# A hybrid SSD and attention block: attention's gate projected by channels, its tiles in another pool, and norm scaling moved to ScalarE

## The chip, the cores and the metric

The kernel runs on one core of a Trainium2 chip. The metric is the device time of one execution in microseconds. TensorE (PE in the profile; PEld is its weight load) multiplies matrices from SBUF into PSUM, VectorE (DVE) and ScalarE (ACT) do elementwise work, GpSimd (POOL) a few small operations, and SyncE (SP) issues the DMAs.

## The reference

One layer, 1024 tokens of 1024 channels, float32. The input is normed and projected; one part goes through a state space scan (SSD), another through differential attention; both are gated, joined, projected out, added to the input and normed.

```python
proj = jnp.einsum('bsd,de->bse', rms_norm(h, norm_gain), w_in)
z_ssd, xbc, dt_raw, q, k, v, z_attn = jnp.split(proj, SPLITS, axis=-1)
...                                   # the scan gives y_ssd
# 8 heads, two maps m each, causal, with a linear bias by distance
p = softmax(where(dist >= 0, q @ k.T * 64**-0.5 - slope * dist, -inf))
w = p[:, :, 0] - lam * p[:, :, 1]
attn = rms_norm(w @ v, subln_gain) * (1.0 - lambda_init)   # over a head's 128 channels
y_attn = attn.reshape(bsz, seq, D_ATTN) * silu(z_attn)
h = h + concatenate([y_ssd, y_attn]) @ w_out
return rms_norm(h, final_norm_gain)
```

## The kernel before, in words

Every projection splits both factors into a high and a low float32r part (hi and lo of the weights, uh and ul of the normed input, which stands with channels on the partitions) and adds three products. `proj_tok` makes 128 tokens by 256 channels: the input is the stationary operand, and each of its 24 matmuls has 256 columns. `proj_ch` makes 128 channels by 512 tokens: the weights are stationary, and each of its 24 matmuls has 512 columns. Results go to one of two PSUM banks with the tag "mm".

After the scan's two groups, attention goes over four pairs p of heads (2p and 2p + 1). In program order a pair is: q and k of the even head (`proj_qk`), v of both heads (`proj_v`), attention of the even head in two halves of 512 tokens (`run`, `attend`), the gate's projection for both heads, q and k of the odd head, and its attention. In the last pair the gate's second half is projected after q and k of the odd head. The gate is silu(z) times two: Tanh on ScalarE (L321), then (tanh + 1) * z on VectorE (L322), in tiles `za` of 512 tokens by 256 channels.

`attend` takes four blocks of 128 queries: scores into PSUM (L557), maximum with bias on VectorE (L563), exponential on ScalarE (L581), combination of both maps on VectorE (L594), transposes on TensorE (L602), eviction on ScalarE (L605), product with v (L609). At the end of a half it leaves `oc`, queries on partitions, and the norm's factor `r` (L614 to L632).

`gate` multiplies `oc` by r and z (L641, per 128 queries), transposes (L647), evicts with the norm's gain g8 (L649), and stores to the DRAM tile `tt_d` (L651), from which the output projection loads its stationary operand. For the last head's first half it also writes hi and lo of the last of the 16 channel tiles (kt = 15) of three token tiles directly (L656, L657). Gates wait in a list and are made during a later half's blocks, at the places given by `at`.

The output projection (L709 to L711) needs the pieces of `tt_d`: `load_t` loads them to `rt` (L701) and splits them into th and tl (L703, L704). Token tiles 0 to 2 are begun while attention of the last head still runs; their loads stand in the program after the last gate projection, at a lowered priority.

Tiles come from SBUF pools by tag. G has 13 slots of 4 KB per partition: x, convolution outputs, `dist`, q and k (six tiles per head), v (two per pair), z, later `tts[2]`, `xr0` and most of the second half of w_out. K has 4 slots of 2 KB: small setup tiles, the scan's state and gate pairs, later `rt` and two residual tiles. H has 5 slots (`oc`, `t`, `tTa`). A planner takes the program with its own simulated costs, hands out slots, and fixes each engine's order before the run; each engine then works through its list, waiting on semaphores.

Of the kernel before, what the change touches and what calls it, by code (L numbers as in the profile page):

```python
# [8 lines left out]
F32 = mybir.dt.float32  # L9
F32R = mybir.dt.float32r  # L10
BF16 = mybir.dt.bfloat16
AF = mybir.ActivationFunctionType
ALU = mybir.AluOpType
AX = mybir.AxisListType

P = 128
# [4 lines left out]
HALF = 512  # L21
# [17 lines left out]
def kernel(  # L39
# [11 lines left out]
    V, A, G, T = nc.vector, nc.scalar, nc.gpsimd, nc.tensor  # L51
# [29 lines left out]
    def ps_mm():  # L81
        return psum.tile([P, HALF], F32, tag="mm", bufs=2, name="mm")
# [9 lines left out]
    def ps_t():  # L92
        return psum.tile([P, HALF], F32, tag="tp", bufs=1, name="tp")
# [66 lines left out]
    g8 = const.tile([P, 1], F32, name="g8")  # L160
# [17 lines left out]
    for half in range(2):  # L178
        for t in range(4 * half, 4 * half + 4):
            ss = sm.tile([P, 1], F32, tag="ss1", name=f"ssx{t}")  # L180
            A.activation(tH([P, D], BF16, "sqx"), x_t[t], AF.Square, accum_out=ss)
            r = rsqrt_mean(ss, 1, 1.0 / D, f"x{t}")
            V.tensor_scalar(x_t[t], x_t[t], r, None, ALU.mult)
        for d in range(ND):
            pt = ps_t() if d == 4 else ps_o() if d == 5 else ps_1()
# [17 lines left out]
    def proj_ch(w, n, half, ps):  # L203

        hi, lo = w
        cut = slice(n * P, (n + 1) * P)
        for d in range(ND):
            T.matmul(ps, hi[:, d, cut], uh[half][:, d, :], start=(d == 0), stop=False)  # L208
            T.matmul(ps, hi[:, d, cut], ul[half][:, d, :], start=False, stop=False)  # L209
            T.matmul(ps, lo[:, d, cut], uh[half][:, d, :], start=False, stop=(d == ND - 1))  # L210
# [113 lines left out]
    def proj_gate_half(w, half, name):  # L324
        z = tG([P, 4, 256], name=name)
        for a in range(2):
            proj_gate(w, 2 * half + a, z[:, 2 * a : 2 * a + 2, :])
        return z
# [5 lines left out]
    for d0, d1 in D3:  # L334
        hi, lo = (tG([P, d1 - d0, NZ], F32R, f"wz_{n}{d0}") for n in ("hi", "lo"))
        for n, raw in enumerate(raw_z0 + [wdt_raw]):
            cut = slice(n * P, min(NZ, (n + 1) * P))
# [186 lines left out]
    def proj_v(p):  # L524
# [9 lines left out]
            vs.append(v)  # L534
        return vs

    def attend(h, half, qkc, vs):

        qs, ks = qkc
        slope = 2.0 ** -(h + 1)  # L540
        vcut = slice((h % 2) * P, (h % 2 + 1) * P)
        po = ps_o()
        sums = sm.tile([P, 2, 4], F32, tag="sums", name=f"sums{h}{half}")
        for ii in range(4):
            i = 4 * half + ii
            n = (i + 1) * P
# [13 lines left out]
            for m in range(2):  # L560
                ps = pss[m]
# [5 lines left out]
                    op0=ALU.add,  # L567
                    op1=ALU.max,
                    scale=1.0,
# [16 lines left out]
                    scale=slope,  # L586
# [11 lines left out]
            for b0 in range(0, i + 1, 4):  # L598
                nb_ = min(4, i + 1 - b0)
                pt = ps_t()  # L600
# [12 lines left out]
        oc = tH([P, HALF], name=f"oc{h}{half}")  # L613
        V.tensor_scalar(oc, po, O_MAX, -O_MAX, ALU.min, ALU.max)  # L614
        ss = sm.tile([P, 4], F32, tag="ss4", name=f"sso{h}{half}")
        for ii in range(4):
# [4 lines left out]
                scale=2.0**-12,  # L621
# [6 lines left out]
        keep = sm.tile([P, 4], F32, tag="keep", name=f"keep{h}{half}")  # L628
        V.scalar_tensor_tensor(keep, ss, SQ_MAX, inv, op0=ALU.is_lt, op1=ALU.mult)
        V.tensor_scalar(ss, ss, SQ_MAX, None, ALU.min)  # L630
        r = rsqrt_mean(ss, 4, 2.0**24 / P, f"o{h}{half}")
# [1 line left out]
        yield oc, r  # L633

    def gate(h, half, normed, z):
        vcut = slice((h % 2) * P, (h % 2 + 1) * P)
        oc, r = normed
        tt = tH([P, HALF], name=f"t{h}{half}")
        for ii in range(4):
            cut = slice(ii * P, (ii + 1) * P)  # L640
            V.scalar_tensor_tensor(  # L641
                tt[:, cut], oc[:, cut], r[:, ii : ii + 1], z[:, ii, vcut], op0=ALU.mult, op1=ALU.mult
            )
        pt = ps_t()
        for ii in range(4):
            cut = slice(ii * P, (ii + 1) * P)
            T.transpose(pt[:, cut], tt[:, cut], ident)  # L647
        tT = tH([P, HALF], name=f"tTa{h}{half}")
        A.activation(tT, pt, AF.Copy, scale=g8)  # L649
        td, k = tt_of(8 + h, 4 * half)  # L650
        dma(td[k], tT)  # L651
        if h == HEADS - 1 and half == 0:
            for t in range(3):
                cut = slice(t * P, (t + 1) * P)
                hi, lo = (x[:, AHEAD_K - 1, :] for x in tts[t][1])
                A.activation(hi, pt[:, cut], AF.Copy, scale=g8)  # L656
                V.scalar_tensor_tensor(lo, pt[:, cut], g8, hi.bitcast(F32), op0=ALU.mult, op1=ALU.subtract)  # L657


    NK = 16  # L660
# [52 lines left out]
    waiting = []  # L713

    def run(h, half, qkc, vs, at):

        unit = attend(h, half, qkc, vs)
        for n in range(4):
            next(unit)
            if n in at and waiting:  # L720
                gate(*waiting.pop(0))
        return next(unit)

    for p in range(HEADS // 2):
        h = 2 * p
        qkc = proj_qk(h)
        vs = proj_v(p)
        even = [run(h, half, qkc, vs, (1,)) for half in range(2)]
        zw = load_w(B_ZA + 2 * p, B_ZA + 2 * p + 1, f"za{p}")
        last = p == HEADS // 2 - 1  # L730
        zs = [proj_gate_half(zw, half, f"za{p}{half}") for half in range(1 if last else 2)]
        qkc = proj_qk(h + 1)
        if last:
            zs.append(proj_gate_half(zw, 1, f"za{p}1"))
        waiting += [(h, half, even[half], zs[half]) for half in range(2)]
        if last:
            xr0 = tiles_out()
            with tc.high_priority(-2000):
                for t in range(3):
                    load_t(t, 0, 4)  # L740
                wo = [load_wo(0)]
        for half in range(2):
            at = (2,) if last and half else (2, 3)
            waiting.append((h + 1, half, run(h + 1, half, qkc, vs, at), zs[half]))
    while waiting:
        gate(*waiting.pop(0))

# [45 lines left out]
    for t in range(NT):  # L793
# [18 lines left out]
        for k, (n, c0, c1) in enumerate(pieces):  # L812
            if t <= 2 and n == 0:
                ps = pss[t]
            else:
                ps = ps_mm()
# [50 lines left out]
```

## Time and profile before

| | |
|---|---|
| median of three runs | 1049.15 us (1048.91 to 1049.41) |
| profiled execution, its own time | 1049.18 us |
| its span, first to last instruction | 1047.4 us |
| TensorE busy | 1021.0 us, 97% |
| VectorE, ScalarE, GpSimd busy | 586.8, 505.7, 114.2 us |
| granted TensorE clock | 0.999 |

Times in a timeline are microseconds from the start of the span. A matmul's duration runs from its start to its modelled end and overlaps the next one's. In a group's row the figures are count, busy time, mean duration in ns, and after the bar the idle time of that engine just before, with what ended it. The scan and what precedes it fill the span up to about 366 us, attention with its projections runs to about 914, and the rest of the output projection to the end.

### The profile page before, as it was taken

To read this page: it belongs to the slowest core of one execution; us is meant where nothing else is said; L and a number is where in the kernel's file an instruction comes from. 1 tells how busy PE (TensorE), PEld (TensorE's weight loads), DVE (VectorE), ACT (ScalarE), POOL (GpSimd) and SP (SyncE) were. 2 spreads that over 40 slices of the span, in tenths; PEclk is the share of its full clock that TensorE was granted. 3 is DMA by queue.
4 is the path that set the end of the run, shared out by engine and by line. 5 is a ranking of instruction groups with operands and counts; after the bars stand their busy time and mean duration, and the time that the engine had idled before them with its cause. 6 is when DMAs were issued, how large, how long until landed. Compare 5 with 4: busy or idle time off the path is not lost.

```text
span 1047.4 us, 16245 instructions
## 1 busy us (share of the span) xinstructions
PE 1021.0 (97%) x6334; PEld 906.2 (87%) x6334; DVE 586.8 (56%) x1285; ACT 505.7 (48%) x1137; POOL 114.2 (11%) x141
## 2 busy tenths in 40 slices
PE   6999999999999999999999999999999999999997
PEld 5988888879988998889998899988998987788886
DVE  6555678755666265573664745637546477462221
ACT  8354367834457354463554544534545565341110
POOL 6000024200223100000000000000002230010000
PEclk9999999999999999999999999999999999999999
DMA  7111224311224212320122121131211433463211
GB/s 291 41 63 41 68 65 131 91 51 61 101 81 121 81 42 61 81 67 25 51 61 61 41 62 62 51 81 41 62 56 52 136 116 129 141 182 115 81 46 41
DMA packets 52085, 84.54 MB, mean 81 GB/s; under 512 B 3932, under 2 KB 30633, under 8 KB 52009
## 3 DMA queue, kind: packets, MB, share of 16 engines
q1 hardware_dynamic: 52008, 83.51, 25.3%
q8 instruction: 50, 0.82, 0.3%
q14 instruction: 27, 0.21, 0.1%
HBM read 62.45 MB, written 12.65 MB: 72 GB/s over the span
## 4 chain that ended last, share of the span: by engine, by line
PE 89%; issue 3%; ACT 3%; DVE 2%; DMA 1%; POOL 1%; POOLq 0%; DVEq 0%; SPq 0%; ACTq 0%
PE mm L208 9%; PE mm L209 9%; PE mm L210 9%; PE mm L217 8%; PE mm L218 8%; PE mm L219 8%; PE mm L709 6%; PE mm L710 6%; PE mm L711 6%; PE o L609 5%; PE S L557 5%; PE S L439 3%; PE tp L602 3%; PE S L448 1%; PE S L452 1%
## 5 line engine op out<-in xcount | busy, mean ns | idle before, releaser
L563 DVE CUSTOM_DVE_ANT_0 s<-S,dist 128x256 f32<-128x256 f32 (+7 forms) x128 | 94.5, 755 | 111.2 <-PE S L557 103.9
L581 ACT ACTIVATE s<-s,small 128x256 f32<-128x256 f32 (+7 forms) x128 | 98.5, 770 | 72.1 <-DVE small L573 71.5
L208 PE MATMUL mm<-uh,hi_qk 128*128 128x512 f32 x256 | 101.5, 397 | 0.0
L210 PE MATMUL mm<-uh,lo_qk 128*128 128x512 f32 x256 | 101.0, 394 | 0.0
L209 PE MATMUL mm<-ul,hi_qk 128*128 128x512 f32 x256 | 100.8, 394 | 0.0
L557 PE MATMUL S<-k,q 128*128 128x512 f32 (+2 forms) x384 | 90.6, 355 | 0.5 <-DVE small L563 0.5
L605 ACT ACTIVATE wT<-tp 128x512 f32<-128x512 f32 (+2 forms) x96 | 46.6, 485 | 77.7 <-PE tp L602 77.2
L609 PE MATMUL o<-v,wT 128*128 128x128 f32 x576 | 79.9, 275 | 2.5 <-ACT wT L605 2.5
L609 PEld LDWEIGHTS o<-v,wT 128*128 128x128 f32 x576 | 74.3, 191 | 6.6 <-ACT wT L605 3.7
L217 PE MATMUL mm<-hi_v,uh 128*128 128x256 f32 x256 | 73.7, 288 | 0.9 <-DVE q L508 0.9
L218 PE MATMUL mm<-lo_v,uh 128*128 128x256 f32 x256 | 73.3, 286 | 0.0
L219 PE MATMUL mm<-hi_za,ul 128*128 128x256 f32 x256 | 73.2, 286 | 0.0
L219 PE MATMUL mm<-hi_v,ul 128*128 128x256 f32 x256 | 73.0, 285 | 0.0
L218 PE MATMUL mm<-lo_za,uh 128*128 128x256 f32 x256 | 72.9, 285 | 0.0
L217 PE MATMUL mm<-hi_za,uh 128*128 128x256 f32 x256 | 72.8, 284 | 0.0
L557 PEld LDWEIGHTS S<-k,q 128*128 128x128 f32 x384 | 64.6, 189 | 9.4 <-DVE small L563 1.4
L210 PEld LDWEIGHTS mm<-uh,lo_qk 128*128 128x128 f32 x256 | 48.1, 188 | 9.8 <-issue 0.2
L208 PEld LDWEIGHTS mm<-uh,hi_qk 128*128 128x128 f32 x256 | 48.1, 188 | 9.1 <-issue 0.2
L209 PEld LDWEIGHTS mm<-ul,hi_qk 128*128 128x128 f32 x256 | 48.2, 188 | 8.7
L217 PE MATMUL mm<-hi_z,uh 128*128 128x256 f32 x192 | 55.2, 287 | 0.0
L594 DVE SCALAR_TENSOR_TENSOR s<-s,small,s 128x128 f32<-128x128 f32 (+3 forms) x64 | 54.2, 848 | 1.6
L219 PE MATMUL mm<-hi_z,ul 128*128 128x256 f32 x192 | 55.0, 287 | 0.0
(217 smaller groups left out, 2631.5 us busy)
## 6 DMA issues: line engine op xcount, KB each, us to landing
m<-acs_d SPq DMA_DIRECT2D x16, 512.0 KB, 4.1
raw_qk<-in_w_blocks_dram SPq DMA_DIRECT2D x16, 512.0 KB, 4.0
q<-q SPq DMA_DIRECT2D x32, 256.0 KB, 2.9
rwo<-in_w_out_dram SPq DMA_DIRECT2D x16, 512.0 KB, 3.6
rt<-tt_d SPq DMA_DIRECT2D x27, 256.0 KB, 3.7
x<-in_x_dram SPq DMA_DIRECT2D x8, 512.0 KB, 6.2
raw_z<-in_w_blocks_dram SPq DMA_DIRECT2D x8, 512.0 KB, 4.1
raw_xs<-in_w_blocks_dram SPq DMA_DIRECT2D x8, 512.0 KB, 4.0
```

What stands on the lines that cost most here:

```text
L208: T.matmul(ps, hi[:, d, cut], uh[half][:, d, :], start=(d == 0), stop=False)
L209: T.matmul(ps, hi[:, d, cut], ul[half][:, d, :], start=False, stop=False)
L210: T.matmul(ps, lo[:, d, cut], uh[half][:, d, :], start=False, stop=(d == ND - 1))
L217: T.matmul(ps, uh[half][:, d, cut], hi[:, d, :], start=(d == 0), stop=False)
L218: T.matmul(ps, uh[half][:, d, cut], lo[:, d, :], start=False, stop=False)
L219: T.matmul(ps, ul[half][:, d, cut], hi[:, d, :], start=False, stop=(d == ND - 1))
L557: T.matmul(os[m], qs[half][m][:, part, qcut], ks[kh][:, m, :width], start=(part == 0), stop=(part == 1))
L563: V.tensor_tensor_reduce(out=s[:, :n], in0=ps[:, :n], in1=dist[:, S - n : S], op0=ALU.add, op1=ALU.max, scale=1.0, scalar=-3.0e38, accum_o ...
L581: A.activation(s[:, :n], s[:, :n], AF.Exp, bias=nb[:, m : m + 1], scale=slope, accum_out=sums[:, m, ii : ii + 1],)
L609: T.matmul(po[:, qcut], wT[:, kb, :], vs[kb // 4][:, kb % 4, vcut], start=(kb == 0), stop=(kb == i))
L709: T.matmul(ps, th[:, k, :], hi, start=(kt == first), stop=False)
L710: T.matmul(ps, th[:, k, :], lo, start=False, stop=False)
```

## The change

The gate's projection goes by channels: `proj_za` makes, for each head and half, 128 channels by 512 tokens with `proj_ch`, as two tiles per head. For the first three pairs the tiles are in pool K, for the last in G. In the last pair the even head's gate is projected before q and k of the odd head, and the odd head's after. Since z now has channels on partitions, `gate` scales `oc` by r alone, on ScalarE, transposes, and multiplies by g8 and z on VectorE as it evicts. The direct hi and lo of kt = 15 are taken from that result in SBUF rather than from PSUM.

```diff
+    def proj_za(w, n, name, keep):
+
+        z = []
+        for half in range(2):
+            z.append((tK if keep else tG)([P, HALF], name=f"{name}{half}"))
+            ps = ps_mm()
+            proj_ch(w, n, half, ps)
+            A.activation(z[half], ps, AF.Tanh, scale=0.5)
+            V.scalar_tensor_tensor(z[half], z[half], 1.0, ps, op0=ALU.add, op1=ALU.mult)
+        return z
...
     def gate(h, half, normed, z):
-        vcut = slice((h % 2) * P, (h % 2 + 1) * P)
         oc, r = normed
         tt = tH([P, HALF], name=f"t{h}{half}")
         for ii in range(4):
             cut = slice(ii * P, (ii + 1) * P)
-            V.scalar_tensor_tensor(
-                tt[:, cut], oc[:, cut], r[:, ii : ii + 1], z[:, ii, vcut], op0=ALU.mult, op1=ALU.mult
-            )
+            A.activation(tt[:, cut], oc[:, cut], AF.Copy, scale=r[:, ii : ii + 1])
...
         tT = tH([P, HALF], name=f"tTa{h}{half}")
-        A.activation(tT, pt, AF.Copy, scale=g8)
+        V.scalar_tensor_tensor(tT, pt, g8, z[half], op0=ALU.mult, op1=ALU.mult)
...
-                A.activation(hi, pt[:, cut], AF.Copy, scale=g8)
-                V.scalar_tensor_tensor(lo, pt[:, cut], g8, hi.bitcast(F32), op0=ALU.mult, op1=ALU.subtract)
+                A.activation(hi, tT[:, cut], AF.Copy)
+                V.tensor_tensor(lo, tT[:, cut], hi.bitcast(F32), ALU.subtract)
...
-        zs = [proj_gate_half(zw, half, f"za{p}{half}") for half in range(1 if last else 2)]
+        zs = [proj_za(zw, 0, f"za{h}", not last)]
+        if not last:
+            zs.append(proj_za(zw, 1, f"za{h + 1}", not last))
         qkc = proj_qk(h + 1)
         if last:
-            zs.append(proj_gate_half(zw, 1, f"za{p}1"))
-        waiting += [(h, half, even[half], zs[half]) for half in range(2)]
+            zs.append(proj_za(zw, 1, f"za{h + 1}", not last))
+        waiting += [(h, half, even[half], zs[0]) for half in range(2)]
...
-            waiting.append((h + 1, half, run(h + 1, half, qkc, vs, at), zs[half]))
+            waiting.append((h + 1, half, run(h + 1, half, qkc, vs, at), zs[1]))
```

## The prediction

> **What bounds the kernel now.** I read the busy times and the 40 slices of the page first, then the chain that ended last.
>
> ```profile
> span 1047.4 us, 16245 instructions
> PE 1021.0 (97%) x6334; PEld 906.2 (87%) x6334; DVE 586.8 (56%) x1285; ACT 505.7 (48%) x1137; POOL 114.2 (11%) x141
> PE   6999999999999999999999999999999999999997
> PE 89%; issue 3%; ACT 3%; DVE 2%; DMA 1%; POOL 1%; POOLq 0%; DVEq 0%; SPq 0%; ACTq 0%
> ```
>
> TensorE is busy in every slice and is nine tenths of the chain; VectorE and ScalarE are half idle. So what shortens TensorE's own list of work shortens the kernel, unless it only opens a hole elsewhere. Next I looked for the holes there are, in stretches of the attention phase (columns: stretch, its length, TensorE's busy time and instructions, granted clock, DMA share, GB/s).
>
> ```profile
> 455.00:470.00 15.00, 13.56 (x78) 1.00 0.30 89
> 590.00:604.00 14.00, 13.20 (x74) 1.00 0.21 59
> 725.00:739.00 14.00, 13.21 (x75) 1.00 0.23 66
> 835.00:870.00 35.00, 34.31 (x191) 1.00 0.31 98
> 870.00:892.00 22.00, 19.75 (x114) 1.00 0.42 135
> 892.00:914.00 22.00, 20.88 (x106) 1.00 0.45 156
> ```
>
> The first three are the seams between head pairs: 1.44, 0.80 and 0.79 us idle, 3.0 in all. The other three are the end of attention: 0.69 + 2.25 + 1.12 = 4.1 us idle. The clock was 1.00 throughout.
>
> **Part 1, the gate's projection.** By tokens it is 4 pairs x 8 token tiles x 24 = 768 matmuls of 256 columns. By channels it is 8 heads x 2 halves x 24 = 384 matmuls of 512 columns, the form that the q/k projection already has. A matmul's listed duration overlaps the next one's, so the price is the distance of starts (columns: start, duration, engine, line). The gate now:
>
> ```profile
> 367.01 0.28 PE L219 MATMUL mm<-hi_za,ul 128*128 128x256 f32 x1
> ...
> 369.17 0.28 PE L219 MATMUL mm<-hi_za,ul 128*128 128x256 f32 x1
> ```
>
> Eighteen steps in 2.16 us, 0.120 each. The q/k projection in an unbroken block, and where attention's work had just come between:
>
> ```profile
> 433.73 0.39 PE L209 MATMUL mm<-ul,hi_qk 128*128 128x512 f32 x1
> ...
> 437.36 0.39 PE L210 MATMUL mm<-uh,lo_qk 128*128 128x512 f32 x1
> ```
> ```profile
> 409.69 0.40 PE L208 MATMUL mm<-uh,hi_qk 128*128 128x512 f32 x1
> ...
> 411.99 0.39 PE L209 MATMUL mm<-ul,hi_qk 128*128 128x512 f32 x1
> ```
>
> Sixteen steps in 3.63 us, 0.227 each; ten in 2.30, 0.230 each. So 768 x 0.120 = 92.2 us becomes 384 x 0.227 = 87.2: **-5.0 us**. With 0.230 throughout it is -3.9, and no row is below 0.227. I take -5.0, since the 0.120 too comes from an unbroken block. The 384 weight loads that go as well lay under matmuls and are worth nothing by themselves; the matmuls were what filled the time.
>
> What a rule would make of it: the Trainium skill, "TensorE: Matmul & The Clock Gate", section "Back-to-back issue gap", gives a warm gap of N / 2.4 + 2.5 ns, so 109.2 ns for 256 columns and 215.8 for 512. By that estimate halving the count saves 83.9 - 82.9 = 1.0 us only. This trace shows about 13 ns beyond N / 2.4 at both widths, not 2.5, and the measured pitch decides.
>
> **Part 2, scaling and gating.** A gate before: four VectorE products, four transposes, one ScalarE copy out of PSUM. After: four ScalarE copies scaled by r, the same transposes, one VectorE product out of PSUM. The rows, first groups (their mean in ns after the comma), then two runs of four:
>
> ```profile
> L641 DVE SCALAR_TENSOR_TENSOR t<-oc,r_o,za 128x128 f32<-128x128 f32 x64 | 18.7, 353 | 0.1
> L649 ACT ACTIVATE tTa<-tp,g 128x512 f32<-128x512 f32 x16 | 10.9, 684 | 19.4 <-PE tp L647 19.4
> L322 DVE SCALAR_TENSOR_TENSOR za<-za,mm 128x512 f32<-128x512 f32 x16 | 10.9, 683 | 5.7 <-ACT za L321 5.7
> L425 ACT ACTIVATE m<-m,acs 128x128 f32<-128x128 f32 x128 | 39.3, 389 | 13.6 <-DMA m<-acs_d 13.6
> ```
> ```profile
> 864.61 1.13 DVE L641 SCALAR_TENSOR_TENSOR t<-oc,r_o,za 128x128 f32<-128x128 f32 x4
> 341.79 1.11 ACT L412 ACTIVATE tT<-o,sg 128x128 f32<-128x128 f32 x4
> ```
>
> Four VectorE products took 1.13 us. Four ScalarE copies with a per-partition scale took 1.11 us reading PSUM; reading SBUF, the nearest row is L425 with 389 ns each, so the four lie between 1.11 and 4 x 0.39 = 1.56. The move out of PSUM is 0.684 on ScalarE against 0.683 on VectorE (L322). A gate's own path changes by -0.02 to +0.43 us. VectorE loses 16 x (1.13 - 0.68) = 7 us of work and ScalarE gains 16 x (1.11 to 1.56 - 0.68) = 7 to 14 us. TensorE's matmuls hide both, with half of either engine idle: I take 0. If the cover were gone at every gate it would cost 16 x 0.43 = 7 us: the copies stand in ScalarE's queue before the next block's exponential (L581) and the eviction of the transposed weights (L605), for which TensorE's L609 waits. That bites only at the seams and the end. The projection's Tanh and product stay 16 and 16 of 128x512. No DMA is added; SP issues the stores of tTa at the same points.
>
> For the last head's first half, hi and lo of three token tiles now come from SBUF:
>
> ```profile
> 891.95 0.37 ACT L656 ACTIVATE th<-tp,g 128x128 fp32r<-128x128 f32 x1 [0.42 <-DVE tl L657]
> 892.35 0.35 DVE L657 SCALAR_TENSOR_TENSOR tl<-tp,g,th 128x128 fp32r<-128x128 f32 x1 [0.43 <-ACT th L656]
> ```
>
> Reading one PSUM tile, the two engines took turns, each waiting 0.42 us for the other. Two such waits of ScalarE can go (-0.8 us at best).
>
> **Part 3, where z lies.** Pool G (13 slots) held two z tiles per pair; pairs 0 to 2 now use pool K (4 slots, four z of half the size). Pair 3 holds four in G instead of two. What a slot of G is worth shows at a seam (two VectorE rows, then TensorE's first filler):
>
> ```profile
> 453.34 0.68 DVE L508 SCALAR_TENSOR_TENSOR q<-mm,q 64x512 fp32r<-64x512 f32 x1 [0.62 <-ACT q L507]
> ...
> 468.85 0.69 DVE L508 SCALAR_TENSOR_TENSOR q<-mm,q 64x512 fp32r<-64x512 f32 x1
> 469.60 0.39 PE L217 MATMUL mm<-hi_v,uh 128*128 128x256 f32 x1 [0.36 <-DVE q L508]
> ```
>
> Two parts of one q projection left PSUM 15.5 us apart. In G at that time, by the code: dist 1, v 2, z 2, four of the running head's q and k, four of the next head's: 13, full. The next head's last q and k tiles wait for the running half's q to be read; both "mm" banks stay taken, and v's projection starts only at 469.60. Without z in G exactly two slots are free. I expect two thirds of the seams' 3.0 us to go: **-2.0 us**, bounds -3.0 (all of it) and 0 (the head's own chain ends there anyway).
>
> In pair 3 the two extra tiles leave G only when head 6 has been gated. They stand before the loads of token tile 2 (G for hi and lo, K for the raw pieces), and the kt = 14 step at the end waits for K too:
>
> ```profile
> 867.26 0.81 SPq L701 DMA_DIRECT2D rt<-tt_d  x2
> 872.27 0.50 PE L709 MATMUL mm<-wo_hi,th 128*128 128x512 f32 x1 [0.53 <-ACT th L703]
> ```
>
> The loads go out behind head 6's gate and TensorE waits for them. Best case -0.8 (above); the other end, +9.5, is rival two. I take **+1.0 us**, near the lower end, since gate and load would be late by a copy or two only.
>
> Sum: -5.0 + 0 - 2.0 + 1.0 = -6.0. The profiled execution took 1049.2 us, 1.8 more than its span and level with the median of 1049.15: **1043.2 us**. All best ends together give -5.0 - 3.0 - 0.8 = -8.8, all worst ends -3.9 + 7 + 9.5 = +12.6.
>
> **Rivals.** *One, no gain.* The TensorE time that goes turns into idle time at the same seams, because attention's chain (VectorE maximum, ScalarE exponential, transposes) sets a pair's end. For it: the seams are idle now. Against it: only 3 us in three seams, and q/k blocks without any attention lie between. It gives -1 to 0 us, about 1048.5; the rule's 1.0 us saving would end there too, with little added chance, as its pitch is not the trace's.
>
> *Two, the end.* Raw pieces of token tile 2 fill K while they wait for G, so the kt = 14 pieces cannot be loaded at 867.26 but only after the last scores of head 7 are read, some 10 us later. TensorE then loses the cover of tile 2's 14 x 3 x 0.227 = 9.5 us of matmuls: -5.0 - 2.0 + 9.5 = +2.5, 1051.7. It decides from a delay beyond 7 us on. Against it: K's other pieces free two slots with the first copy.
>
> *Three, K is not idle.* Token tile 0's first pieces take two of K's slots long before they are used:
>
> ```profile
> 326.59 0.99 SPq L701 DMA_DIRECT2D rt<-tt_d  x2
> 821.62 1.96 ACT L703 ACTIVATE th<-rt 128x512 fp32r<-128x512 f32 x4
> ```
>
> If they keep those places, four z share two slots, the other two z hold both "mm" banks until gates free them, and q/k groups lose their double buffer: up to 12 groups x 2.7 us (two evictions each on ScalarE and VectorE in turn, as L649 and L322 4 x 0.68) = 33 us, half of it filled by attention, an estimate: -5 + 16 = +11, 1060. Against it, the planner seems to hand out slots in program order, in which z of pairs 0 to 2 stand before these loads:
>
> ```profile
> 399.01 0.14 DVE L632 TENSOR_TENSOR r_o<-r_o,keep 128x4 f32<-128x4 f32 x1
> ...
> 431.83 0.69 DVE L614 TENSOR_SCALAR oc<-o 128x512 f32<-128x512 f32 x1 [4.20 <-PE o L609]
> 432.56 1.14 DVE L641 SCALAR_TENSOR_TENSOR t<-oc,r_o,za 128x128 f32<-128x128 f32 x4
> ```
>
> The first gate's operands were ready at 399.2, yet its tile of pool H came only after that of the next half, which stands before it in the program. Then the loads simply start later, still before 821.
>
> *Four, more.* All seams and half of the end fill: -5.0 - 3.0 - 2.0 = -10, 1039.
>
> **How the numbers follow.** Forecast, 1041 to 1046: 0.60. Rival four 0.14, one 0.11, two 0.08, three 0.07. What a measurement of this kernel can tell from no change is 0.2%, 2.1 us. Faster 0.74 (forecast and four), same 0.11, slower 0.15. The range 1038.5 to 1049.5 leaves out rival two and three and a little of four, 0.19; the likeliest case alone is 1041 to 1046.
>
> **What would show it.** Right: gate matmuls as 384 rows of 128x512 at 0.227 from start to start; TensorE's busy time near 1016; v's filler directly behind the next head's last q/k with no L508 pair 15 us apart; four ScalarE copies of 1.1 to 1.6 us per gate; z written without waiting for a gate. Wrong: ScalarE's Tanh (L321) or VectorE's product of z waiting on K, q/k groups alone in one PSUM bank, the first loads of token tile 0 still at 326, the kt = 14 step far later behind head 6's gate, or L609 waiting longer for L605.

## The result, and the profile after

The changed kernel is slower: 1055.67 us median (1054.22 to 1056.65, six runs) against 1049.39 (1048.91 to 1050.78, six runs) for the kernel before on the same chip, ratio 1.0057, 95% interval 1.0044 to 1.0070. The prediction, 1043.2 in a range of 1038.5 to 1049.5, was wrong by 12.5 us and in its sign. The profiled execution has a span of 1054.3 us at a granted clock of 0.997, 6.9 us longer than before's. One execution further down, of e12_prio_pool, took 1460.38 us at a granted clock of 0.655; ratios leave it out.

The page of the changed kernel, the lines that answer to those of before:

```profile
span 1054.3 us, 15478 instructions
PE 1021.5 (97%) x5950; PEld 887.9 (84%) x5950; DVE 587.7 (56%) x1237; ACT 514.9 (49%) x1185; POOL 113.1 (11%) x141
PE   6999999999999999999999999999999988899997
PE 90%; DVE 3%; ACT 3%; issue 1%; DMA 1%; POOL 1%; SPq 0%; POOLq 0%; DVEq 0%; ACTq 0%
```

There are 384 fewer matmuls, and three slices, the 33rd to the 35th, have fallen from 9 to 8: the stretch from about 843 to 922 us. The windows of before again, and the three stretches that turn out to matter (columns as in the prediction: stretch, length, TensorE's busy time and instructions, granted clock, DMA share, GB/s):

```profile
455.00:470.00 15.00, 15.00 (x107) 1.00 0.35 111
590.00:604.00 14.00, 14.00 (x109) 1.00 0.24 76
725.00:739.00 14.00, 14.00 (x109) 1.00 0.15 50
807.00:819.00 12.00, 9.96 (x67) 1.00 0.30 86
835.00:870.00 35.00, 30.77 (x164) 1.00 0.43 139
870.00:892.00 22.00, 19.79 (x109) 1.00 0.44 141
892.00:914.00 22.00, 21.07 (x114) 1.00 0.45 156
914.00:918.00 4.00, 1.36 (x9) 1.00 0.17 66
918.00:922.00 4.00, 4.00 (x11) 0.57 0.00 0
```

The seams are full, as forecast. The end is not: 4.23 us idle in 835 to 870 (before 0.69), 2.64 in 914 to 918, and behind that a stretch at a clock of 0.57. The new gate projection and the gate's new steps:

```profile
503.12 0.40 PE L209 MATMUL mm<-ul,hi_za 128*128 128x512 f32 x1
...
506.78 0.39 PE L210 MATMUL mm<-uh,lo_za 128*128 128x512 f32 x1
```
```profile
L652 ACT ACTIVATE t<-oc,r_o 128x128 f32<-128x128 f32 x64 | 20.7, 389 | 3.8 <-DVE r_o L643 3.8
L658 DVE SCALAR_TENSOR_TENSOR tTa<-tp,g,za 128x512 f32<-128x512 f32 x16 | 12.0, 750 | 16.8 <-PE tp L656 16.5
```

Sixteen steps in 3.66 us, 0.229 each: the price of part 1 was right to one per cent. The pieces of part 2 cost about what was said: four copies 20.7 / 16 = 1.29 us, the product 0.750 instead of 0.683.

To see where the time went I use one measure for all kernels: the sum of what the distance between two successive matmul starts exceeds the usual one for their shape (0.111 us for 128 columns or fewer, 0.120 for 256, 0.125 for 272, 0.175 for 384, 0.227 for 512), in us. It counts idle time and matmuls slowed by a low clock alike, and it is uncertain by about 1, since some records are missing. Each column is one traced execution. The last row counts the stretches between 765 and 930 us in which the clock record of that trace has TensorE at half rate; each is 3.41 us long and so costs up to 1.7. (e13 and e15, which leave out some matmuls, come further down.)

| stretch | before | after | e1_pack | e3_pack_vec | e9_prio | e18 | e16 | e13 | e15 |
|---|---|---|---|---|---|---|---|---|---|
| 330 to 765 | 16.4 | 15.2 | 15.2 | 12.5 | 13.4 | 15.2 | 11.7 | 16.4 | 15.4 |
| 765 to 810 | 1.3 | 2.5 | 1.2 | 1.2 | 1.1 | 2.0 | 1.2 | 1.3 | 1.4 |
| 810 to 870 | 2.8 | 8.9 | 7.9 | 10.0 | 7.3 | 8.2 | 5.1 | 5.6 | 6.5 |
| 870 to 900 | 5.4 | 4.7 | 4.3 | 4.0 | 4.1 | 5.7 | 4.5 | 7.2 | 5.6 |
| 900 to 930 | 0.2 | 4.7 | 2.0 | 1.9 | 4.5 | 0.2 | 1.2 | 0.2 | 0.2 |
| half rate | 0 | 1 | 0 | 1 | 1 | 1 | 0 | 1 | 2 |

The gate projection's own steps, where one follows another, took 0.1197 us on the mean before and 0.2288 after, which makes 91.9 and 87.9 us. So about 4 us of work went (5.0 forecast), and 11 us came behind 765 us, from the last pair on: idle time, but for up to 1.7 us of half rate. Four links in the trace of the changed kernel account for it; the experiments test the first, the third and the fourth.

*Head 7's q and k wait for slots of G.* SyncE's queue (columns: start, length, queue, line, operation, count), the changed kernel:

```profile
787.14 14.25 SPq L511 DMA_DIRECT2D q<-q  x3
817.49 0.47 SPq L511 DMA_DIRECT2D q<-q  x1
828.16 2.72 SPq L699 DMA_DIRECT2D rwo<-in_w_out_dram  x2
```

The fourth copy of q comes at 817.49, though head 7's q and k matmuls were through at 807.5; both "mm" banks stay taken, and the window 807 to 819 has 2 us idle. The copies of the kernel before are no earlier:

```profile
814.85 0.47 SPq L511 DMA_DIRECT2D q<-q  x1
818.04 0.47 SPq L511 DMA_DIRECT2D q<-q  x1
```

But there head 7's q and k matmuls ran until 818.8, so TensorE had work while the copies waited. The changed kernel was 11 us ahead with these matmuls, and the lead was gone with the wait: head 7's gate projection starts at 819.05, the last gate half of the kernel before at 818.98.

*The first piece of w_out waits for head 7's gate.* Its hi and lo take the place of the input's first half, uh and ul. Projected by tokens, the last gate half read only the second half of the input; by channels every head's gate reads both. ScalarE's first copies of w_out, before and after:

```profile
803.88 1.99 ACT L693 ACTIVATE wo_hi<-rwo 128x1024 fp32r<-128x1024 f32 x2
```
```profile
824.59 2.01 ACT L702 ACTIVATE wo_hi<-rwo 128x1024 fp32r<-128x1024 f32 x2 [0.69 <-PE mm L209]
831.77 1.06 ACT L702 ACTIVATE wo_hi<-rwo 128x1024 fp32r<-128x1024 f32 x1 [3.68 <-DMA rwo<-in_w_out_dram]
843.11 1.06 ACT L702 ACTIVATE wo_hi<-rwo 128x1024 fp32r<-128x1024 f32 x1 [5.62 <-DMA rwo<-in_w_out_dram]
850.34 1.06 ACT L702 ACTIVATE wo_hi<-rwo 128x1024 fp32r<-128x1024 f32 x1 [3.68 <-DMA rwo<-in_w_out_dram]
```

*ScalarE then stands before these loads in its list*, 13 us in the three rows, and head 7's exponentials behind them.

*The last piece of w_out's second half takes the slot of head 7's second z tile*, which is free only after the gate's product, now behind the transposes. VectorE, then TensorE:

```profile
912.35 1.23 DVE L703 TENSOR_TENSOR wp_lo<-rwo,wp_hi 128x1024 fp32r<-128x1024 f32 x1 [1.04 <-ACT wp_hi L702]
915.20 0.75 DVE L658 SCALAR_TENSOR_TENSOR tTa<-tp,g,za 128x512 f32<-128x512 f32 x1 [1.62 <-PE tp L656]
916.52 1.22 DVE L703 TENSOR_TENSOR wp_lo<-rwo,wp_hi 128x1024 fp32r<-128x1024 f32 x1
```
```profile
917.79 0.60 PE L719 MATMUL mm<-wp_lo,th 128*128 128x512 f32 x1 [2.64 <-DVE wp_lo L703]
918.19 0.63 PE L720 MATMUL mm<-wp_hi,tl 128*128 128x512 f32 x1
918.62 0.63 PE L718 MATMUL mm<-wp_hi,th 128*128 128x512 f32 x1
```

Before, the four products stood ahead of that gate's transposes and the last two pieces followed at 909.80 without a gap:

```profile
908.74 1.14 DVE L641 SCALAR_TENSOR_TENSOR t<-oc,r_o,za 128x128 f32<-128x128 f32 x4
909.80 2.35 DVE L694 TENSOR_TENSOR wp_lo<-rwo,wp_hi 128x1024 fp32r<-128x1024 f32 x2
```

After the change TensorE waits 2.64 us and then starts matmuls 0.426 us apart instead of 0.227.

### The profile page after: what moved, and what is told of

The parts are those of the page before. It is cut to its first block, busy times and chain, and to the rows that moved or that the text cites. A ratio compares the mean times of both kernels' runs of the same rounds, so it can differ in the third digit from the quotient of the medians.

```text
span 1054.3 us, 15478 instructions
## 1 busy us (share of the span) xinstructions
PE 1021.5 (97%) x5950; PEld 887.9 (84%) x5950; DVE 587.7 (56%) x1237; ACT 514.9 (49%) x1185; POOL 113.1 (11%) x141
## 3 DMA queue, kind: packets, MB, share of 16 engines
q1 hardware_dynamic: 52008, 83.51, 25.2%
## 4 chain that ended last, share of the span: by engine, by line
PE 90%; DVE 3%; ACT 3%; issue 1%; DMA 1%; POOL 1%; SPq 0%; POOLq 0%; DVEq 0%; ACTq 0%
PE mm L208 12%; PE mm L209 12%; PE mm L210 12%; PE S L568 5%; PE o L620 5%; PE mm L218 5%; PE mm L219 5%; PE mm L217 5%; PE mm L718 5%; PE mm L720 5%; PE mm L719 5%; PE S L439 3%; PE tp L613 3%; PE S L448 1%; PE S L452 1%
## 5 line engine op out<-in xcount | busy, mean ns | idle before, releaser
L568 PE MATMUL S<-k,q 128*128 128x512 f32 (+2 forms) x384 | 93.8, 358 | 4.2 <-DVE small L574 4.1
L173 POOL TENSOR_SCALAR m_o<-sso 128x4 f32<-128x4 f32 x16 | 3.1, 193 | 504.8 <-DVE sso L641 389.6
L719 PE MATMUL mm<-wp_lo,th 128*128 128x512 f32 (+1 forms) x144 | 53.3, 370 | 2.6 <-DVE wp_lo L703 2.6
L218 PE MATMUL mm<-lo_z,uh 128*128 128x256 f32 x192 | 54.9, 286 | 0.0
```

Source lines behind the costliest of these rows:

```text
L218: T.matmul(ps, uh[half][:, d, cut], lo[:, d, :], start=False, stop=False)
L568: T.matmul(os[m], qs[half][m][:, part, qcut], ks[kh][:, m, :width], start=(part == 0), stop=(part == 1))
L719: T.matmul(ps, th[:, k, :], lo, start=False, stop=False)
```

## The experiments

Times are medians; ratios are to the kernel before on the same chip, with their 95% intervals. The theories are named by letters in the expectations. A: pair 3's two extra tiles in G make the loss, by what then waits for slots. B: the scaling copies on ScalarE hold up what stands behind them. C: the planner made a worse order of the new work, by chance. P, formed after the first runs: the last pair is bound by the attention of heads 6 and 7, so that TensorE time saved turns into idle time there.

**e1_pack**: both halves of a head's z in one 4 KB slot, so pair 3 takes two slots of G, not four.

```diff
+        both = None if keep else tG([P, 2, HALF], name=name)
...
-            z.append((tK if keep else tG)([P, HALF], name=f"{name}{half}"))
+            z.append(tK([P, HALF], name=f"{name}{half}") if keep else both[:, half, :])
```


> The changed kernel, but in the last pair both halves of a head's z share one 4 KB tile of pool G, so that z takes two slots there, as before the change, not four. Theory A (the two extra slots of G in the last pair delay head 7's q and k tiles, and with them SP's queue, the w_out loads and ScalarE): the loss of about 11 us after 800 us goes, 1042 to 1047 us, no third q store 14 us behind the first. Theory B (ScalarE's scaling copies stand before the exponentials and delay attention's chain): 1054 to 1057, as the changed kernel. Theory C (a chance of the planner's order, no single cause): anywhere between 1044 and 1058.

Measured 1050.55 us, 1.0009 (1.0001 to 1.0018): 5.1 us faster than the changed kernel. Of what single edits to the changed kernel undid, pair 3's slots are the largest part. Less came back than theory A expected: 810 to 870 still has 7.9 us. Head 7's last k tile leaves PSUM at 816.20, nine microseconds after its matmuls.

**e2_before_short** and **e2b_before_hold**: the kernel before with two more tiles of G held in the last pair; in e2b their readers stand behind gates.

```diff
+            held += [tG([P, 2, HALF], name=f"held{n}") for n in range(2)]
...                                                                    # for both tiles
+            G.memset(held[n][:, 0, 0:4], 1.0)
...
+            G.tensor_copy(junk2, held[0 if h == HEADS - 2 else 1][:, 0, 0:4])                        # e2, in gate
+            G.tensor_tensor(junk2, tT[:, 0:4], held[0 if h == HEADS - 2 else 1][:, 0, 0:4], ALU.mult)  # e2b
```


> The kernel before, with two further 4 KB tiles of pool G held in the last pair, from ahead of head 7's q and k projection, one until head 6's second gate and one until head 7's first (four elements each written and read by GpSimd). All projections and gates are those of before. Theory A: slower than before by 6 to 12 us, 1055 to 1062, with head 7's second q half leaving PSUM late. Theory B: 1049 to 1050, since ScalarE's list is untouched. Theory C: anywhere.

> The kernel before, with two more tiles of the pool G (4 KB slots) taken when the last pair's gate projection takes its own; each is written once by GpSimd and read by GpSimd after a gate (head 6's second, head 7's first), so that the last pair has two slots fewer for head 7's q and k, as in the changed kernel. (In e2_before_short the reads ran at 776.85 us, right behind the writes, so the slots were held for 4 us only and that run tested nothing.) Theory A (the shortage of slots alone makes the loss): head 7's second q group is copied some 10 to 20 us later, the loads of w_out behind it on SyncE's queue with it, and the time is 1053 to 1059 us (the 11 us of stalls that the change shows after 765 us, less what its other parts add). Theory C (the loss comes of the order that the planner makes of the new work): the order of the old work is made for the slots that are there, 1048 to 1051.

e2: 1049.0, 0.9994 (0.9985 to 1.0003). It held the slots for 4 us only and says nothing. e2b: 1057.47, 1.0077 (1.0064 to 1.0089). Two slots fewer cost 8 us in the old kernel too. But not by the way I expected: head 7's last q copies keep their times (815.90 and 818.69; before 814.85 and 818.04). The late tiles are the end's, as in the changed kernel's fourth link, though not behind a gate's product: the last two pieces of w_out are converted at 918.32 instead of 909.80, and TensorE waits for them (e2b, TensorE's wait in the timeline, then the window behind it, with all engines and the clock of 0.63):

```profile
920.74 0.55 PE L712 MATMUL mm<-wp_lo,th 128*128 128x512 f32 x1 [2.24 <-DVE wp_lo L696]
```
```profile
920.00:924.00 4.00, 3.26 (x8) 2.64 (x9) 1.35 (x3) 0.00 (x0) 0.00 (x0) 0.63 0.17 66
```

**e4_pack_allG**: e1_pack with z of all four pairs in G.

```diff
-        zs = [proj_za(zw, 0, f"za{h}", not last)]
+        zs = [proj_za(zw, 0, f"za{h}", False)]
...                                        # the other two calls likewise; e1's packing as above
```


> As the packed kernel, but z of all four pairs in pool G, two slots a pair as before the change; pool K is not used for z. It takes the seams' gain away and leaves the projection's. Theory A, with the seams worth what the traces show (6.3 us ahead at the last pair, of which 4 are three quarters of the projection's saving): 2 to 3 us slower than the packed kernel, 1045 to 1049, v's projection again starting late at the seams. If the seams are worth nothing: equal to the packed kernel within 1 us. Theory B: 1054 to 1057.

Measured 1058.89, 1.0091 (1.0076 to 1.0106). With the slots that before used, everything else of the change costs 9.5 us, and the move to K is worth 8.3, not 2. By the measure 330 to 765 has 25.2 us (one half-rate stretch among them) against 16.4. By the code a slot that was freed by the first step of a gate is now freed by its last, and the rows show TensorE waiting for that last step; no run separates this from the other differences (e4, waits of TensorE in 455 to 765):

```profile
PE tp L614 <- DVE tTa L659: 3.8, 3, 1.3
PE tp L614 <- ACT wT L617: 2.9, 1, 2.9
```

**e3_pack_vec** and **e11_before_scale**: the scaling's engine, undone in e1_pack, and done alone in the kernel before.

```diff
-            A.activation(tt[:, cut], oc[:, cut], AF.Copy, scale=r[:, ii : ii + 1])        # e3, from e1
+            V.tensor_scalar(tt[:, cut], oc[:, cut], r[:, ii : ii + 1], None, ALU.mult)
...
-            V.scalar_tensor_tensor(tt[:, cut], oc[:, cut], r[:, ii : ii + 1], z[:, ii, vcut], ...)   # e11, from before
+            A.activation(tt[:, cut], oc[:, cut], AF.Copy, scale=r[:, ii : ii + 1])
...                                                                   # t4 is tt by query blocks
+        V.tensor_tensor(t4, t4, z[:, :, vcut], ALU.mult)
```


> e1_pack with the scaling by r back on VectorE (four multiplications of 128x128 by r in place of four ScalarE copies). Theory B (ScalarE's four copies of 1.27 us a gate hold up evictions and exponentials behind them): 1047 to 1049.5, 1 to 3 us faster than e1_pack's 1050.55. Theory A and theory P (below, e7): no difference beyond 1 us either way; a loss up to 2 us would say that VectorE is the tighter engine there.

> The kernel before with one part of the change alone: the scaling by r as four ScalarE copies a gate, and then one VectorE product of 128x512 with the gate; projection, pools and the place of the gate's product as before. Theory B (the scaling on ScalarE costs by itself, 2.5 us between e1_pack and e3_pack_vec): 1050.5 to 1053. The prediction priced it at nothing: 1049 to 1050.

e3: 1048.09, 0.9985 (0.9976 to 0.9994), 2.5 us better than e1_pack. e11: 1050.79, 1.0012 (1.0004 to 1.0021), 1.3 worse than before. The scaling on ScalarE is not free. In e3_pack_vec the measure of 330 to 765 falls from 15.2 to 12.5: stalls inside the pairs, which the change had brought, shrink. Of 534 to 538 TensorE was idle for 0.80 us in the changed kernel and is not in e3; of 664 to 675 it was idle for 0.68 and is for 0.35. In e11 810 to 870 has 4.0 us against 2.8.

**e6_rwo_pool**: the changed kernel with the first eight loads of w_out on GpSimd's queue.

```diff
-            dma(raw, src.rearrange("(a p) c -> p a c", p=P))
+            (nc.gpsimd.dma_start if n == 0 else dma)(raw, src.rearrange("(a p) c -> p a c", p=P))
```


> The changed kernel with the first eight w_out loads issued from GpSimd's queue rather than SP's; nothing else is moved. If SP's queue carries the delay on (the w_out loads stand behind the q copy that waits for a slot of G, and ScalarE then waits for w_out ahead of its exponentials): the idle time between 831 and 870 us falls from 6.9 us towards the 2.1 of before, 1050 to 1053 us; the idle time between 807 and 819 stays. If the queue is not the link: 1054 to 1057.

Measured 1051.78, 1.0018 (1.0009 to 1.0027): 3.9 us faster, as expected: by the measure 831 to 870 fell from 6.7 to 4.4 us, and 807 to 819 stayed as it was. Yet it is not for the reason given. The third load still goes out at 830.44, no earlier than the 828.16 above: it needs a slot that GpSimd frees by converting the first two pieces (done at 828.1 and 830.5 in both kernels), and now stands behind both conversions in GpSimd's list. What changed is ScalarE's list, which now reaches the pieces when they have landed or nearly so (the only two waits for them that are left):

```profile
853.59 1.06 ACT L702 ACTIVATE wo_hi<-rwo 128x1024 fp32r<-128x1024 f32 x1 [0.34 <-DMA rwo<-in_w_out_dram]
856.91 1.06 ACT L702 ACTIVATE wo_hi<-rwo 128x1024 fp32r<-128x1024 f32 x1 [1.25 <-DMA rwo<-in_w_out_dram]
```

So the loss went with the waits in ScalarE's order, the third link; GpSimd's order changed with it.

**e7_pack_early** and **e8_before_early**: head 6's gates earlier, to bring kt = 14 forward.

```diff
-            at = (2,) if last and half else (2, 3)
+            at = (2,) if last and half else (0, 1) if last else (2, 3)
```


> e1_pack with head 6's two gates run after the first and second query block of head 7's first half instead of after the third and fourth. Theory P: in e1_pack the two accumulations of the output projection that hold both mm banks run through their steps kt 0 to 13 by 852.7 us, then TensorE has no other work than head 7's attention until kt=14 at 868.6 (4.9 us idle in 850 to 870, before 1.6), so what was saved earlier is given back there. With the gates earlier kt=14 follows some 10 to 15 us sooner, the attention is covered again, and 2 to 5 us come back: 1045.5 to 1048.5. Rival: the idle time is that of ScalarE's queue (copies of w_out pieces, scaling copies) and is not removed by other work for TensorE: 1050 to 1052.

> The kernel before with the same edit as e7_pack_early (head 6's gates after the first and second query block of head 7's first half). Theory P: before has filler until 862.9 and lacks it only until 870.4 (1.3 us idle), so the edit is worth 0 to 1.5 us here: 1047.5 to 1049.5. If it gains as much as in e7 (2 to 5 us), the edit is a better order for either kernel and says nothing on what the change lost.

e7: 1055.78, 1.0061 (1.0048 to 1.0073). e8: 1059.17, 1.0086 (1.0073 to 1.0100). Both kernels lose, 5 and 10 us: kt = 14 does come sooner (863.8 and 861.8), but the work that it releases is then missing behind the last exponentials (5.2 and 4.9 us idle in 885 to 900; e1_pack 1.9, before 2.9), and the granted clock of that window is 0.77 and 0.89. The edit is a bad order for either and tells nothing of what the change lost.

**e9_prio**, **e10_before_prio**, **e12_prio_pool**: head 7's attention raised in the planner's priority, in e3_pack_vec and in the kernel before; e12 adds e6's edit.

```diff
+            with tc.high_priority(300 if last else 0):
                 waiting.append((h + 1, half, run(h + 1, half, qkc, vs, at), zs[1]))
```


> e3_pack_vec with head 7's attention and the gates that run with it raised in the planner's priority (300). Nothing is computed otherwise; the order written for TensorE changes: the projection of head 7's gate and the output projection's steps are spread between head 7's query blocks, where e3_pack_vec has 60 of those steps close together and then a stretch of attention with hardly any. Theory P (what is left between e3_pack_vec's 1048.1 and the forecast 1043 is idle time of TensorE, 4.3 us in 810 to 835 and 4.6 in 850 to 870 against 0.7 and 1.6 before, from how the planner mixes the last pair's work, and no cost of the change's own instructions): 1044 to 1046.5. Rival (ScalarE's queue or the loads of w_out set that idle time): 1047.5 to 1049.

> The kernel before with the same priority for head 7's attention, as the control of e9_prio. Theory P: before already mixes that work evenly (0.7 and 1.6 us idle in the two windows), so 1048 to 1050.5; a gain of 2 us or more here would say that the priority is a better order for either kernel, and e9's gain no measure of what the change lost.

> e9_prio with the first eight loads of w_out on GpSimd's queue, so that they do not stand behind the copies of head 7's q. If a wait behind those copies is still left after the packing, 1 to 3 us faster than e9_prio (1042.5 to 1045); if the packing removed it, the same within 1 us.

e9: 1046.99, 0.9978 (0.9969 to 0.9986), the fastest kernel of the study, but only 1.1 us of the 2 to 4 expected. e10: 1051.11, 1.0016 (1.0007 to 1.0025), 0.6 above what was expected. e12: 1048.54, 0.9991 (0.9982 to 1.0000): 1.5 slower than e9, which neither branch had. The order is a part, not the whole: in its trace e9 still has 17.0 us between 765 and 930, against 9.7 before. That trace is of e9's longest execution, 1049.07 us, and its one half-rate stretch accounts for up to 1.7 of the 17.0; the other ten took 1046.34 to 1047.85 at granted clocks of 0.998 and 0.999.

**e13_before_less3**, **e15_before_less0**, **e16_packvec_more0**: a known amount of TensorE work taken or added.

```diff
-            zs.append(proj_gate_half(zw, 1, f"za{p}1"))                        # e13
+            zs.append(proj_gate_half(zw, 1, f"za{p}1", ND // 2))
...
-        zs = [proj_gate_half(zw, half, f"za{p}{half}") for half in ...]          # e15
+        zs = [proj_gate_half(zw, half, f"za{p}{half}", ND // 2 if p == 0 and half else ND) for half in ...]
...
-            proj_ch(w, n, half, ps)                                            # e16, from e3
+            proj_ch(w, n, half, ps, 2 if name == "za1" and half else 1)
```


> The kernel before, with half of the matmuls of the last pair's second gate half left out (48 of 128x256, 5.8 us at 0.120; that gate is then wrong). If TensorE bounds the last pair (the forecast's step): 1043 to 1045. If the attention chain of heads 6 and 7 bounds it (theory P): most of the 5.8 us turns into idle TensorE time between 810 and 900, 1047.5 to 1050, and the order written for TensorE gets the same stretch of attention without other work as e1_pack's.

> The kernel before, with half of the matmuls of the first pair's second gate half left out (48 of 128x256, 5.8 us; that gate is then wrong). Here the saving lies 400 us ahead of the end and moves everything behind it, attention too: by the forecast's step 1043 to 1045, and by theory P too, since P speaks of work saved beside head 6's and 7's attention. If this does not arrive either (1047.5 or more), work saved anywhere between the scan and the end is lost and P is too narrow.

> e3_pack_vec with one gate projection of the first pair (head 1's second half) doing every step twice, 24 matmuls of 128x512 more, 5.4 us at 0.227 (that gate is then wrong). If TensorE bounds all from there to the end: 1053 to 1054.5. If e3_pack_vec's lead is lost in the tail anyway, the added work costs less than half, 1048 to 1050.5.

e13: 1047.22, 0.9973 (0.9963 to 0.9983): 2.4 of 5.8 us arrive. e15: 1047.37, 0.9967 (0.9955 to 0.9980): 2.2 of 5.8, although the work lay 400 us ahead of the end. Both lie between their two branches. The traces say where the rest went (810 to 870 and 870 to 900, e13 and then e15):

```profile
810.00:870.00 60.00, 57.43 (x342) 1.00 0.42 131
870.00:900.00 30.00, 25.99 (x134) 0.94 0.45 147
```
```profile
810.00:870.00 60.00, 57.28 (x348) 0.97 0.39 118
870.00:900.00 30.00, 27.34 (x148) 0.94 0.47 156
```

In e13 most of it is idle time: by the table 14.3 us between 765 and 930 against 9.7 before, one half-rate stretch of up to 1.7 among them. In e15 it is the clock. TensorE ran at half rate from 863.8 to 867.2 and from 891.1 to 894.5, up to 3.4 us, which is nearly all of the 4.0 that the same rows have more than before. Its five executions fit that: three took 1047.4 to 1047.6 us at a granted clock of 0.995, two 1045.6 and 1045.9 at 0.997, so that 3.7 to 4.0 of the 5.8 arrived there. So e15 does not show that work saved early is lost in bare attention.

e16: 1048.59, 0.9983 (0.9974 to 0.9992): 5.4 us more work cost 0.5 us beside e3_pack_vec. This takes the sum's first step apart. TensorE in 765 to 810 and 810 to 870, e3_pack_vec and then e16:

```profile
765.00:810.00 45.00, 45.00 (x235) 1.00 0.27 73
810.00:870.00 60.00, 56.16 (x312) 0.97 0.33 107
```
```profile
765.00:810.00 45.00, 45.00 (x237) 1.00 0.24 68
810.00:870.00 60.00, 57.85 (x330) 1.00 0.38 121
```

The added work fills what was idle: by the table 17.1 us between 765 and 930 become 12.0, of which up to 1.7 are the half rate that only e3's trace has (clock 0.97 above). In the traces head 6's last scores start at 815.7 (e3_pack_vec) and at 806.6 before, though head 6's first start ten microseconds earlier, at 758.3 against 768.4: the order gives the time gained to projections, and the attention of heads 6 and 7, with less other work left beside it, sets the end.

**e17_split_prio**: e9_prio with head 6's z in K.

```diff
-        zs = [proj_za(zw, 0, f"za{h}", not last)]
+        zs = [proj_za(zw, 0, f"za{h}", True)]
```


> e9_prio with head 6's gate in the pool K, as the first three pairs have it, and head 7's packed in G: one G slot more while head 7's q and k are projected. In e1_pack and e9_prio head 7's last k tile is copied at 816.2 and 814.5, 9 to 10 us after its matmuls, with both mm banks held meanwhile; with the slot it should follow its matmuls by 806 to 812 and the 1.3 to 2 us idle in 810 to 835 should go: 1045 to 1047. If the idle time only moves to later windows, the same as e9_prio's 1047.0 within 1 us; if K's slots are then missed by the loads of the projected token tiles, slower, 1048 to 1050.

Measured 1052.97, 1.0027 (1.0018 to 1.0036), beyond what was expected for missed slots. Head 7's last k tile is out by 813, 6 us sooner, but the loads of token tiles through K go out in twos until 841, and 810 to 870 has 12.0 us by the measure, one half-rate stretch among them (e9 7.3). A slot gained in one pool was lost in the other.

**e18_after_lastK** and **e19_prio_lastK**: head 7's second z half in K, in the changed kernel and in e9_prio.

```diff
-            z.append((tK if keep else tG)([P, HALF], name=f"{name}{half}"))                          # e18
+            z.append((tK if keep or (name == "za7" and half) else tG)([P, HALF], name=f"{name}{half}"))
...                                                        # e19: the same on top of e9's packing
```


> The changed kernel with one tile moved: the second half of head 7's gate lies in the pool K instead of G, so that the last piece of w_out finds its slot before the last gate's product. If that slot is what the end waits for, the wait of 2.64 us and the 1.8 us of matmuls at the lower clock go, and with one more slot for head 7's q and k up to 3 us more: 1048 to 1051.5 (the changed kernel 1055.7). If K's four slots are then missed by the loads of the projected token tiles, or the end waits for another piece at the same time: 1054 or more.

> e9_prio with head 7's first gate half alone in a G slot and the second in K. If the last piece's slot makes the wait of 2.5 us at 910.84 and the low clock behind it (0.57 from 912 to 916, 1.7 us): 1042.5 to 1044.5, about what the prediction gave for the whole change. If the tail is bound by head 6's and 7's attention alone (theory P), the time stays within 1.5 us of e9_prio's 1047.0.

e18: 1051.40, 1.0017 (1.0008 to 1.0025): 4.3 us faster than the changed kernel by one tile's place. The last piece of w_out no longer stands behind the product, and the wait and the low clock of the end are gone (e18; another half-rate stretch of its trace, from 870.1, stands behind a gap of 1.69 us):

```profile
908.71 1.23 DVE L703 TENSOR_TENSOR wp_lo<-rwo,wp_hi 128x1024 fp32r<-128x1024 f32 x1 [1.15 <-ACT wp_hi L702]
913.07 0.75 DVE L658 SCALAR_TENSOR_TENSOR tTa<-tp,g,za 128x512 f32<-128x512 f32 x1 [3.14 <-PE tp L656]
```
```profile
914.00:918.00 4.00, 4.00 (x19) 1.00 0.62 192
918.00:922.00 4.00, 4.00 (x20) 1.00 0.60 195
```

e19: 1049.56, 0.9997 (0.9988 to 1.0006), 2.6 slower than e9_prio, which neither branch had. There too the wait went (0.1 us in 900 to 930 by the measure, e9's trace 4.5), but 810 to 870 has 11.8 us instead of 7.3. Which order the planner makes of the last pair is worth several microseconds either way, and no kernel tried has both ends right.

## Why the prediction was wrong

**Part 1's price was right, its place in the sum was not.** The 384 steps took 0.227 to 0.229 us, and about 4 us of matmuls went. The formula that the prediction quotes beside its sum from the Trainium skill, "TensorE: Matmul & The Clock Gate", section "Back-to-back issue gap", stands there for a matmul by itself, not for a stream of them; the sum did not use it. That each microsecond taken from TensorE's list comes off the end was the step that failed first: 5.4 us added in e16 cost 0.5, and of 5.8 us taken from the kernel before 2.4 arrived in e13. TensorE at 97% and in nine tenths of the chain had looked like proof; but a list that is full because other work is mixed into attention empties where that work is used up. Rival one said so with the right mechanism (attention's chain) at the wrong place, the seams, and held it for 0.11. The clock takes its share besides: idle gaps bring stretches at half rate, most of what was lost in e15, and the prediction has no term for them.

**Part 2, priced 0.** The copies took 1.29 us a gate (1.11 to 1.56 forecast), the product 0.750 (0.683). The scaling on ScalarE cost 2.5 us (e1_pack to e3_pack_vec) or 1.3 alone (e11). The prediction named the seams and the end as the places where the cover is missing; e3 gets most of its time back inside the pairs instead (534 to 538, 664 to 675), where TensorE's list was taken to be covered. That gating behind the transposes frees z later was not in the sum at all; e4_pack_allG and e18_after_lastK bear on it.

**Part 3, the seams, -2.0.** They are full, and no pair of L508 stands 15 us apart there: the whole 3.0 went. But the table's first row fell by 1.2 us only, since the stalls inside the pairs came in their place; with the scaling back on VectorE it fell by 3.9. So the term was right for the pools alone, and the scaling took much of it. The sign itself moved to the last pair, where the two parts of q left PSUM at 800.22 and 816.77 (before 814.14 and 817.32).

**Part 3, pair 3, +1.0.** This term failed. I looked for the shortage in K and at kt = 14; that step starts at 872.6 against 870.4, 2 us late, so rival two fell, and rival three too, as token tile 0's first load moved to 738.7. The shortage was in G, for head 7's q and k and for w_out's last piece. I had counted G at a seam, 13 of 13, and did not count it again for pair 3. Packing is worth 5.1 us, one tile's move 4.3; both act on the same slots, and no run has both in the changed kernel. And I did not see that a gate by channels keeps the input's first half in use until head 7's gate, 20 us longer for w_out's first piece. That link is in the rows; no run undid it alone.

TensorE's busy time did not fall to 1016 but stayed at 1021.5. A listed duration overlaps the next one's, so it reaches into the gap behind and was a poor witness for the work.

What stays open: how much of the last pair's idle time belongs to the attention chain itself and how much to the planner's order, which is made anew for every edit. e9_prio and e19_prio_lastK move 1 to 3 us by the order alone; 1043 was not reached.

## What to carry to other kernels

A saturated engine's saving counts only if the work that it covers is not then left bare: before summing, take a few microseconds of its work out and see what arrives, and read the granted clock of the windows before calling what is missing idle time. For every buffer that a change writes, reads or frees at another step, ask which tile takes its place next, and who waits for that tile, in each stage anew. A step moved behind another engine's work holds its input's slot and its own engine's list for that time, even where its duration is the same.

## What the runs showed of the hardware that I had not expected

A gap of two to three microseconds in TensorE's work can cost more than itself. After 2.64 us of waiting at 917.79 the granted clock was 0.57 for 918 to 922, with eight starts about 0.426 us apart, 1.7 us more; e9_prio, e2b_before_hold, e4_pack_allG and e15_before_less0 each show a window of 0.50 to 0.63 behind a gap of 2.2 to 2.9 us. But not every one is followed by it: in e17_split_prio the clock was 1.00 behind 2.34 us at 831.24.

The clock records show why like gaps differ. In the twenty traces every stretch at half rate between 100 and 930 us is 3.41 us long, or twice that, and within a trace the changes of rate lie whole multiples of 3.41 us apart, as on a raster. I summed TensorE's idle time in each window of that raster. All eleven windows with 1.9 us or more were followed by half rate, and no window at full rate with 1.58 or less was; between these, five were and five were not. The 2.34 us of e17 fall on two windows, the fuller with 1.85. So several small gaps in one window can cost as much as a single long one: e13's 1.63 us in 887.9 to 891.3 did.

The Trainium skill, "TensorE: Matmul & The Clock Gate", section "What's actually happening", has half the rate after at least one idle window of about 3.4 us, and has the window run freely, without a new start when the kernel starts. The rate (0.426 against 0.227 us) and the window's length agree with the traces; but a window did not have to be idle throughout, 1.9 us of 3.41 were enough here.
